# Attention operands turned through DRAM by one write and one read, with the keys in another order on the partitions

## The chip, the core and the metric

The kernel runs on one core of one Trainium2 chip. The metric is the device time of one execution in microseconds (us). It is given as the median of the timed runs; beside it there is one profiled execution with its trace, whose own time and span are given below.

## The reference, cut to what matters

The model is a decoder trunk of two layers over 272 tokens (16 learned "meta" tokens and 256 of the sequence), with a width of 2048, 16 heads of 128 and an MLP of 8192. Layer 0 is a softmax attention with a forget gate, layer 1 a stick-breaking attention.

```python
for qs, qe in query_blocks(L):          # (0,16), (16,144), (144,272)
    s = einsum('bqhd,bkhd->bhqk', q[:, qs:qe], k[:, :qe]) * scale + decays   # layer 0
    p = softmax(where(mask, s, -inf))
    out = einsum('bhqk,bkhd->bqhd', p, v[:, :qe])
    # layer 1: a = exp(log_sigmoid(z) + suffix sums of log_sigmoid(-z)), strictly causal, out = a @ v
h = h + out @ w_o
h = h + square(relu(rms_norm(h) @ w_up)) @ w_down        # in both layers
```

The sum over the keys k in the last `einsum` doesn't depend on the order in which the keys are taken, as long as the probabilities and the values are in the same order.

## The kernel before, in words

**Layout.** The residual stream is kept with features on the partitions (`hT`, 16 chunks of 128 features by 272 tokens). Every large product is split into parts of reduced precision: a weight block becomes `whi` (L210, on ScalarE, ACT) and `wlo` (L211, on VectorE, DVE), an activation becomes `sp.hi` and `sp.lo`, and three products are summed in place of one (hi·hi, hi·lo, lo·hi).

**Groups.** `gemm_group` makes 512 output features: four blocks of 512 contracted features (`kb` 0 to 3), four output chunks (`m`), four chunks of 128 (`kc`) in a block and three products make 192 products on TensorE (PE). The groups are counted by `u`: 1 to 12 are q, k and v of layer 0 (for four sets `g` of four heads), 13 to 16 its output projection, 17 to 48 its MLP, 49 to 52 the queries of layer 1, 53 to 60 its keys and values, 61 to 64 its output projection and 65 to 96 its MLP. With `t0 = 16` (u = 49 to 52 and from 61) a product is 256 tokens wide, in the others 272. Some products are "widened": they take `sp.wide`, which has 6 columns of zeros behind the 256, so that they write 262 columns, of which 256 are read.

**Attention.** The scores of a head come out with queries on the partitions. The product with the values needs the keys there, for the probabilities and for the values. Both are turned in two steps: VectorE transposes blocks of 32 by 32 (L474, L389), and a trip through DRAM moves the blocks to their partitions. For a pair of heads `pr` (two pairs in a set of four heads), `turn_probabilities` writes to `p_dram[pr]` and `probabilities_back` reads it into `raw`; `scratch` writes to `v_dram[pr]` and `values_read` reads it back into the same tile `turned`. Before the change each write is four DMAs, one for each quarter `a` of the partitions, and the read is one DMA of 2 KB (values) or 3 KB (probabilities) in a row for each partition. Then `values_back` splits the values (`v0` by L377 on ACT and L378 on DVE, `v1` by L409 on ACT). Only when these are done can `weighted` and L812 (L618 in layer 0) make `po` on PE. After that L822 adds the share of the last 16 keys (`own`, copied by L818 on ACT) and `put_split` writes the heads' chunks of `ao` (named x_o; L466 on ACT, L467 on DVE), which the output projection reads.

**The last heads.** The attention of the last four heads of a layer has no later group of its own kind to lie in. It lies in the first group of the output projection (u = 13 and u = 61), at places that are written out by hand: `last_heads(turned, reads, uses, places, ...)` gives the product numbers behind which the values are read, behind which they are split, and at which the two pairs of heads stand on PE. Products 144 to 191 of that group (`kb` = 3) read the chunks of just these heads: chunks 12 and 13 (the first pair) from product 144 on, chunks 14 and 15 (the second pair) from product 168 on.

**The order.** A scheduler sets the order on each engine at build time; `behind` ties a DMA or a split to a place among the products. Each engine works in that order. A DMA that reads from DRAM waits on its issuing queue (POOL's, SP's or ACT's) until the write has landed, and all that is issued behind it waits too. Small pieces (the meta tokens, the last 16 keys) go through `c_dram` and `m_dram` on the same queues.

Of the kernel before, what the change touches and what calls it, by code (L numbers as in the profile page):

```python
# [33 lines left out]
def yoco_kernel(ctx: ExitStack, tc: tile.TileContext, hT_in, gains, b_f, w_f, w_qkv0, w_o0, w_up, w_dn,  # L34
# [180 lines left out]
    def gemm_group(wblk, sp, t0, evac, before={}, after={}, load_x=None, between={}):  # L215
# [7 lines left out]
        for kb in range(4):  # L223
# [16 lines left out]
            for kcs, ms in runs:  # L240
# [6 lines left out]

                wide = [(0, 0, 0), (1, 0, 1), (2, 1, 1)] if t0 and u % 4 == 1 else []
                if u == 61:
# [142 lines left out]
    def scratch(t, products, queues=(nc.gpsimd, nc.gpsimd)):  # L392
        for pr in range(2):
            y = t[:, pr].rearrange("p (c x) -> p c x", c=4)
            for a in range(4):
                ins = queues[pr].dma_start(v_dram[pr].rearrange("c j a x -> a j c x")[a], y[32 * a:32 * a + 32])
                behind(ins, products[pr])

    def values_read(t, pr, read, queue=nc.gpsimd):
        ins = queue.dma_start(t[:, pr], v_dram[pr].rearrange("c j a x -> (c j) (a x)"))  # L400
        behind(ins, read)
        return ins.ins
# [66 lines left out]
    def turn_probabilities(s, raw, pr, queue):  # L469

        y = raw[:, :768].rearrange("p (c h b i) -> p c h b i", c=4, h=2, b=3)
        for i in range(2):
            for b, o in enumerate((0, 144, 144 + P)):
                nc.vector.transpose(y[:, :, i, b, :], s[:, 2 * pr + i, o:o + P].rearrange("p (c k) -> p c k", c=4))  # L474
        y = y.rearrange("p c h b i -> p c (h b i)")
        for a in range(4):
            queue.dma_start(p_dram[pr].rearrange("c j a x -> a j c x")[a], y[32 * a:32 * a + 32])

    def probabilities_back(pps, places, queue):
        for pr, at in enumerate(places):  # L480
            raw, p0 = pps[pr]
            behind(queue.dma_start(raw[:, :768], p_dram[pr].rearrange("c j a x -> (c j) (a x)")), issued[at])

# [258 lines left out]
    for g in range(4):  # L742
# [43 lines left out]
        turned = squares(vT, "pp", f"1_{g}")  # L786
        if g < 3:
            scratch(turned, issued[-2:])
        else:
            scratch(turned, (issued[-20], issued[-1]), (nc.gpsimd, nc.scalar))  # L790

# [47 lines left out]

    box["last"] = last_heads(turned, (36, 60), (84, 116), (120, 146), "1_3", nc.gpsimd, pair1, corner1)  # L840

# [11 lines left out]
    def to_token_major():  # L853
        t = squares(hT[:, 12:, M:], "pp", "h")
        scratch(t, issued[-2:])
        return t
# [131 lines left out]
```

## Time and profile before

| | us |
|---|---|
| median of 3 runs | 2265.85 (2265.61 to 2266.42) |
| profiled execution, its own time | 2264.61 |
| span of that execution's trace | 2262.9 |
| busy: PE, PE weight load | 2255.1, 2247.0 |
| busy: DVE, ACT, POOL | 1355.1, 1056.6, 120.5 |
| DMA | 435.94 MB, 193 GB/s in the mean |

The profile is one execution. Its page gives the busy time of each engine, the time slice by slice, and the chain of work that ended last; the trace behind it answers by line, by tile, by wait and in order of time. In an answer in order of time a row has the start, the time until the last of its instructions ended, the engine, the line of the kernel and the operation, `out<-in`, and in brackets the idle time ahead of it and what ended that. PE's instructions overlap, so that a run of products goes forward by less than the sum of their durations; it is read from one start to the next.

### The profile page before, as it was taken

The numbers are of one execution on the slowest core, as the hardware profiler recorded it, in microseconds if no ns is written. First come the engines' busy times: TensorE is split into PE (matmuls) and PEld (weight loads), VectorE is DVE, ScalarE is ACT, GpSimd is POOL, SyncE is SP. The second block draws the span as 40 slices with busy tenths as digits, with TensorE's granted clock in tenths as the row PEclk, the third lists the DMA queues.
The fourth block names the chain that finished last, engine by engine and source line by source line (L and its number), as shares of the span: only waits on it lengthen the run. The fifth ranks groups of instructions, "written<-read, shape, count | busy, mean of one in ns | idle before, by whom it ended". The sixth has DMA issues, their size and how long they took to land.

```text
span 2262.9 us, 45001 instructions
## 1 busy us (share of the span) xinstructions
PE 2255.1 (100%) x18785; PEld 2247.0 (99%) x18785; DVE 1355.1 (60%) x1989; ACT 1056.6 (47%) x1440; POOL 120.5 (5%) x236
## 2 busy tenths in 40 slices
PE   9999999999999999999999999999999999999998
PEld 9999999999999999999999999999999999999998
DVE  7777676554455455455566688766555555555555
ACT  6444445453354344344444455555544543543554
POOL 1321210000000000000000011200000000001001
PEclk9999999999999999999999999999999999999999
DMA  7766765555555555555555566665656656566664
GB/s 242 238 201 192 227 208 170 186 169 184 179 177 180 175 176 185 173 184 178 170 192 183 180 220 219 213 218 188 198 186 197 198 192 197 186 197 209 197 199 141
DMA packets 131852, 435.94 MB, mean 193 GB/s; under 512 B 18528, under 2 KB 26352, under 8 KB 131648
## 3 DMA queue, kind: packets, MB, share of 16 engines
q1 hardware_dynamic: 122112, 413.57, 56.1%
q0 software_dynamic: 6640, 15.80, 2.3%
q10 hardware_dynamic: 2896, 3.69, 0.5%
q8 instruction: 147, 2.41, 0.4%
q14 instruction: 57, 0.47, 0.1%
HBM read 419.22 MB, written 13.78 MB: 191 GB/s over the span
## 4 chain that ended last, share of the span: by engine, by line
PE 98%; DMA 1%; DVE 0%; issue 0%; ACT 0%; POOL 0%; SPq 0%; POOLq 0%; ACTq 0%
PE acc L177 96%; PE po L415 0%; PE pz L415 0%; PE ps L415 0%; DMA raw<-w_o 0%; DMA turned<-v_dram 0%; DMA raw<-w_qkv 0%; PE pz L764 0%; PE ps L541 0%; DVE wlo L211 0%; PE po L618 0%; PE po L812 0%; ACT whi L210 0%; PE pf L346 0%; POOL ob L887 0%
## 5 line engine op out<-in xcount | busy, mean ns | idle before, releaser
L211 DVE TENSOR_TENSOR wlo<-raw,whi 128x1024 fp32r<-128x1024 f32 (+1 forms) x774 | 928.4, 1215 | 693.1 <-ACT whi L210 685.9
L210 ACT ACTIVATE whi<-raw 128x1024 fp32r<-128x1024 f32 (+1 forms) x774 | 796.7, 1049 | 984.6 <-PE acc L177 947.3
L177 PE MATMUL acc<-x_m,whi 128*128 128x272 f32 (+1 forms) x4096 | 642.9, 281 | 0.0
L177 PE MATMUL acc<-x_u,whi 128*128 128x272 f32 (+1 forms) x3968 | 626.0, 281 | 0.0
L177 PEld LDWEIGHTS acc<-x_m,whi 128*128 128x128 f32 x4096 | 565.7, 188 | 0.1
L177 PEld LDWEIGHTS acc<-x_u,whi 128*128 128x128 f32 x3968 | 550.1, 188 | 0.0
L177 PE MATMUL acc<-x_m,wlo 128*128 128x272 f32 (+1 forms) x2048 | 440.7, 281 | 0.0
L177 PE MATMUL acc<-x_u,wlo 128*128 128x272 f32 (+1 forms) x1984 | 431.5, 281 | 0.0
L177 PE MATMUL acc<-x_a,whi 128*128 128x272 f32 (+1 forms) x2048 | 352.3, 285 | 0.2 <-ACT whi L210 0.2
L177 PEld LDWEIGHTS acc<-x_m,wlo 128*128 128x128 f32 x2048 | 323.2, 188 | 0.0
L177 PEld LDWEIGHTS acc<-x_u,wlo 128*128 128x128 f32 x1984 | 315.1, 188 | 0.0
L177 PEld LDWEIGHTS acc<-x_a,whi 128*128 128x128 f32 x2048 | 300.2, 188 | 1.5 <-issue 0.9
L177 PE MATMUL acc<-x_a,wlo 128*128 128x272 f32 (+1 forms) x1024 | 252.9, 285 | 0.0
L177 PE MATMUL acc<-x_kv,whi 128*128 128x272 f32 x1024 | 193.2, 288 | 0.0
L177 PEld LDWEIGHTS acc<-x_a,wlo 128*128 128x128 f32 x1024 | 175.4, 188 | 0.6 <-issue 0.4
L177 PE MATMUL acc<-x_o,whi 128*128 128x272 f32 (+1 forms) x1024 | 162.4, 282 | 0.5 <-ACT x_o L466 0.3
L177 PEld LDWEIGHTS acc<-x_kv,whi 128*128 128x128 f32 x1024 | 160.7, 188 | 0.0
L177 PE MATMUL acc<-x_kv,wlo 128*128 128x272 f32 x512 | 146.9, 287 | 0.0
L177 PEld LDWEIGHTS acc<-x_o,whi 128*128 128x128 f32 x1024 | 142.1, 188 | 0.8 <-ACT x_o L466 0.5
L295 DVE TENSOR_TENSOR hT<-acc,hT 128x272 f32<-128x272 f32 (+1 forms) x156 | 67.3, 432 | 73.2 <-PE acc L177 73.0
L177 PE MATMUL acc<-x_o,wlo 128*128 128x272 f32 (+1 forms) x512 | 110.4, 281 | 0.0
L177 PEld LDWEIGHTS acc<-x_kv,wlo 128*128 128x128 f32 x512 | 96.4, 188 | 0.0
(221 smaller groups left out, 1120.9 us busy)
## 6 DMA issues: line engine op xcount, KB each, us to landing
raw<-w_up SPq DMA_DIRECT2D x256, 512.0 KB, 4.0
raw<-w_dn SPq DMA_DIRECT2D x256, 512.0 KB, 4.3
raw<-w_qkv SPq DMA_DIRECT2D x92, 512.0 KB, 4.4
raw<-w_o SPq DMA_DIRECT2D x64, 512.0 KB, 4.4
raw<-w_kv SPq DMA_DIRECT2D x64, 512.0 KB, 4.3
raw<-w_q SPq DMA_DIRECT2D x32, 512.0 KB, 4.3
v_dram<-turned POOLq DMA_DIRECT2D x56, 64.0 KB, 3.9
turned<-v_dram POOLq DMA_DIRECT2D x14, 256.0 KB, 5.3
```

The costliest lines, as they stand in the source:

```text
L177: ins = nc.tensor.matmul(*args, **kw).ins
L210: on_act = nc.scalar.activation(hp, src, AF.Copy)
L211: on_dve = nc.vector.tensor_tensor(out=lp, in0=src, in1=hp.bitcast(F32), op=ALU.subtract)
L295: nc.vector.tensor_tensor(out=hT[:, c, t0:], in0=acc, in1=hT[:, c, t0:], op=ALU.add)
```

## The change

Four things change. (1) In both trips through DRAM (`scratch` with `values_read`, `turn_probabilities` with `probabilities_back`) the write is one DMA over all 128 partitions in the order in which they lie, and the read picks four pieces (512 bytes each for values, 768 for probabilities) for each partition; the keys come to lie on the partitions as (j c) and no longer (c j). The trip of the final tokens (`to_token_major`) keeps the four writes and the old order. (2) The write of the last heads' second pair in layer 1 goes to POOL's queue; before, it went to ACT's. (3) The places of the last heads of layer 1 change: splits behind products 70 and 106 (before: 84 and 116), pairs at 112 and 132 (before: 120 and 146). (4) Seven more products are widened: three in u = 62, two each in u = 49 and u = 65.

```diff
@@ -245,7 +245,9 @@
                     products = [(kc, m, *pair) for m in ms for kc in kcs for pair in pairs]
                 left = {m: 3 * len(kcs) for m in ms}
 
-                wide = [(0, 0, 0), (1, 0, 1), (2, 1, 1)] if t0 and u % 4 == 1 else []
+                wide = [(0, 0, 0), (1, 0, 1), (2, 1, 1)] if t0 and (u % 4 == 1 or u == 62) else []
+                if t0 and 2 in before:
+                    wide = wide + [(2, 0, 0), (2, 1, 0)]
                 if u == 61:
                     wide = wide + [(3, 2, 0), (3, 2, 1), (3, 3, 1)]
                 for kc, m, part, x in products:
@@ -391,13 +393,11 @@
 
     def scratch(t, products, queues=(nc.gpsimd, nc.gpsimd)):
         for pr in range(2):
-            y = t[:, pr].rearrange("p (c x) -> p c x", c=4)
-            for a in range(4):
-                ins = queues[pr].dma_start(v_dram[pr].rearrange("c j a x -> a j c x")[a], y[32 * a:32 * a + 32])
-                behind(ins, products[pr])
+            ins = queues[pr].dma_start(v_dram[pr].rearrange("a j c x -> (a j) (c x)"), t[:, pr])
+            behind(ins, products[pr])
 
     def values_read(t, pr, read, queue=nc.gpsimd):
-        ins = queue.dma_start(t[:, pr], v_dram[pr].rearrange("c j a x -> (c j) (a x)"))
+        ins = queue.dma_start(t[:, pr].rearrange("p (a x) -> p a x", a=4), v_dram[pr].rearrange("a j c x -> (j c) a x"))
         behind(ins, read)
         return ins.ins
 
@@ -472,14 +472,12 @@
         for i in range(2):
             for b, o in enumerate((0, 144, 144 + P)):
                 nc.vector.transpose(y[:, :, i, b, :], s[:, 2 * pr + i, o:o + P].rearrange("p (c k) -> p c k", c=4))
-        y = y.rearrange("p c h b i -> p c (h b i)")
-        for a in range(4):
-            queue.dma_start(p_dram[pr].rearrange("c j a x -> a j c x")[a], y[32 * a:32 * a + 32])
+        queue.dma_start(p_dram[pr].rearrange("a j c x -> (a j) (c x)"), raw[:, :768])
 
     def probabilities_back(pps, places, queue):
         for pr, at in enumerate(places):
             raw, p0 = pps[pr]
-            behind(queue.dma_start(raw[:, :768], p_dram[pr].rearrange("c j a x -> (c j) (a x)")), issued[at])
+            behind(queue.dma_start(raw[:, :768].rearrange("p (a x) -> p a x", a=4), p_dram[pr].rearrange("a j c x -> (j c) a x")), issued[at])
 
     def split_probabilities(raw, p0):
         return split(p0.rearrange("p x i q -> p x (i q)").rearrange("p x (m y) -> p x m y", m=8),
@@ -784,10 +782,7 @@
         gemm_group(w_kv[2 * g + 1], xc, 0, lambda m, acc: evac_kv(m, acc, vT))
         probabilities_back(pps, (140, 184), nc.sync)
         turned = squares(vT, "pp", f"1_{g}")
-        if g < 3:
-            scratch(turned, issued[-2:])
-        else:
-            scratch(turned, (issued[-20], issued[-1]), (nc.gpsimd, nc.scalar))
+        scratch(turned, issued[-2:] if g < 3 else (issued[-20], issued[-1]))
 
         def corner1(pm_sb, read=None, g=g, vT=vT, pps=pps):
             for pr in range(2):
@@ -837,7 +832,7 @@
                 own1(box["small"], product)
             finish1(pr, po, box["small"][3])
 
-    box["last"] = last_heads(turned, (36, 60), (84, 116), (120, 146), "1_3", nc.gpsimd, pair1, corner1)
+    box["last"] = last_heads(turned, (36, 60), (70, 106), (112, 132), "1_3", nc.gpsimd, pair1, corner1)
 
     xm, norm_m = out_proj(w_o1, ao, M, G_M1, "m1", box.pop("last"))
 
@@ -852,7 +847,10 @@
 
     def to_token_major():
         t = squares(hT[:, 12:, M:], "pp", "h")
-        scratch(t, issued[-2:])
+        for pr in range(2):
+            y = t[:, pr].rearrange("p (c x) -> p c x", c=4)
+            for a in range(4):
+                behind(nc.gpsimd.dma_start(v_dram[pr].rearrange("c j a x -> a j c x")[a], y[32 * a:32 * a + 32]), issued[-2 + pr])
         return t
 
     def tokens_back(t):
```

The new form of the trip lets the scheduler order some instructions in another way. Three places follow. In the rows a name ends in the buffer's numbers.

On POOL, at the last heads of layer 1 (the tile `turned_3`, its DRAM buffers `v_dram_156` for the first pair and `v_dram_157` for the second, and between them the small pieces `pmq_3` and `pk_vc_3`), before:

```order
L440 DMA c_dram<-pkT_3_16875 32x4x16
L120 CAST x_m_17147<-pad 128x16x6
L396 DMA v_dram_156<-turned_3_17129 32x4x128 x4
L445 DMA pmq_3_17259<-c_dram 128x16
L433 COPY pk_vc_3_17268<-vT_3_16878 128x4x16 x2
L400 DMA turned_3_17129<-v_dram_156 128x512
L400 DMA turned_3_17129<-v_dram_157 128x512
```

The same place on POOL now:

```order
L440 DMA c_dram<-pkT_3_16785 32x4x16
L120 CAST x_m_17051<-pad 128x16x6
L396 DMA v_dram_156<-turned_3_17039 128x512
L445 DMA pmq_3_17163<-c_dram 128x16
L433 COPY pk_vc_3_17172<-vT_3_16788 128x4x16 x2
L396 DMA v_dram_157<-turned_3_17039 128x512
L400 DMA turned_3_17039<-v_dram_156 128x4x128
L400 DMA turned_3_17039<-v_dram_157 128x4x128
```

The first pair's write is one row and no longer four DMAs; the second pair's write, which stood on ACT, stands behind the two copies `pk_vc_3`, and both reads come after it.

On PE, in u = 61, around the second pair of the last heads (`po_3_1`, between the products with `whi` and `wlo` of block `kb`_half), before:

```order
L177 MATMUL acc_2_17151<-x_o_14583,wlo_2_1_17300 128x256
L177 MATMUL acc_3_17152<-x_o_14583,wlo_2_1_17300 128x256
L415 MATMUL po_3_1_17389<-p_3_1_16861,v_1_3_1_17384 128x256 x3
L812 MATMUL po_3_1_17389<-raw_p_3_1_16853,v_1_3_1_17385 128x128
L415 MATMUL po_3_1_17389<-p_3_1_16861,v_1_3_1_17384 128x256 x3
L812 MATMUL po_3_1_17389<-raw_p_3_1_16853,v_1_3_1_17385 128x128
L177 MATMUL acc_0_17149<-x_o_14583,whi_3_0_17374 128x256
L177 MATMUL acc_1_17150<-x_o_14583,whi_3_0_17374 128x256
```

And now:

```order
L177 MATMUL acc_2_17055<-x_o_14535,whi_2_1_17203 128x256
L177 MATMUL acc_3_17056<-x_o_14535,whi_2_1_17203 128x256
L415 MATMUL po_3_1_17267<-p_3_1_16774,v_1_3_1_17262 128x256 x3
L807 MATMUL po_3_1_17267<-raw_p_3_1_16766,v_1_3_1_17263 128x128
L415 MATMUL po_3_1_17267<-p_3_1_16774,v_1_3_1_17262 128x256 x3
L807 MATMUL po_3_1_17267<-raw_p_3_1_16766,v_1_3_1_17263 128x128
L177 MATMUL acc_0_17053<-x_o_14535,whi_2_1_17203 128x256
L177 MATMUL acc_1_17054<-x_o_14535,whi_2_1_17203 128x256
```

The second pair stood behind product 143, right ahead of block 3; it now stands behind product 131, twelve products ahead of that block. The first pair stands behind product 111; before, it began behind product 120 and was cut in two by ten products.

On POOL, behind the first set of heads of layer 0 (`turned_0`, and the trip of the meta tokens through `m_dram` to `vm_sb`), before:

```order
L396 DMA v_dram_157<-turned_0_1206 32x4x128 x4
L445 DMA pmq_0_943<-c_dram 128x16
L433 COPY pk_vc_1199<-vT_0_161 128x4x16 x2
L400 DMA turned_0_1206<-v_dram_156 128x512
L460 DMA m_dram<-vt_0_1488 32x8x32 x4
L400 DMA turned_0_1206<-v_dram_157 128x512
L462 DMA vm_sb_1202<-m_dram 128x2x128
```

And now:

```order
L445 DMA pmq_0_937<-c_dram 128x16
L426 COPY pk_vm_1191<-vT_0_161 128x128
L433 COPY pk_vc_1193<-vT_0_161 128x4x16 x2
L396 DMA v_dram_157<-turned_0_1200 128x512
L400 DMA turned_0_1200<-v_dram_156 128x4x128
L400 DMA turned_0_1200<-v_dram_157 128x4x128
L460 DMA m_dram<-vt_0_1476 32x8x32 x4
L462 DMA vm_sb_1196<-m_dram 128x2x128
```

Both reads of the values stand ahead of the four writes to `m_dram` now. On PE the product that reads `vm_sb` (`pom`, L600) stands at the start of u = 5; before, it stood behind 33 products of that group.

## The prediction, made before the changed kernel was run

> **What bounds the kernel now.** I read the page first. TensorE is busy for the whole span, and the chain of work that ended last is TensorE's own.
>
> ```profile
> PE 2255.1 (100%) x18785; PEld 2247.0 (99%) x18785; DVE 1355.1 (60%) x1989; ACT 1056.6 (47%) x1440; POOL 120.5 (5%) x236
> ...
> PE 98%; DMA 1%; DVE 0%; issue 0%; ACT 0%; POOL 0%; SPq 0%; POOLq 0%; ACTq 0%
> ```
>
> Since a busy PE can hide short stops, I asked next for PE's waits.
>
> ```profile
> PE idle L61 <- DVE mean_w L57: 1.1, 1, 1.1
> PE pr_fin L177 <- DVE fin L900: 0.8, 1, 0.8
> PE acc L177 <- ACT x_o L466: 0.3, 1, 0.3
> PE acc L177 <- ACT whi L210: 0.2, 1, 0.2
> PE acc L177 <- DVE x_o L467: 0.2, 1, 0.2
> ```
>
> All waits come to 2.6 us. The first two are the start and the tail, which the change doesn't touch. Two are for x_o: the output projection of layer 1 waits for its last heads. The chain in order of time gives the pace of the products.
>
> ```profile
> 423.83 756.84 PE acc L177 x6144
> 1567.20 671.86 PE acc L177 x5891
> ```
>
> That is 756.84 / 6144 = 0.123 us for a product of 272 columns and 671.86 / 5891 = 0.114 us for one of 256. With this pace I looked for lost time in PE's rows in order of time, in u = 61, from its first product to the place behind the last heads.
>
> ```profile
> 1464.43 1.08 PE L177 MATMUL acc<-x_o,whi 128*128 128x262 f32 x8
> ...
> 1481.43 1.07 PE L177 MATMUL acc<-x_o,wlo 128*128 128x256 f32 x8
> 1482.47 0.84 PE L415 MATMUL po<-p,v 128*128 128x256 f32 x3
> ...
> 1484.38 1.18 PE L177 MATMUL acc<-x_o,whi 128*128 128x256 f32 x8 [0.26 <-ACT x_o L466]
> 1485.75 1.18 PE L177 MATMUL acc<-x_o,whi 128*128 128x256 f32 x8 [0.20 <-DVE x_o L467]
> ```
>
> A pair that waits for nothing is seen in a middle group of layer 1, from its first product to the next pair's:
>
> ```profile
> 1324.79 0.52 PE L415 MATMUL po<-p,v 128*128 128x256 f32 x3
> ...
> 1325.87 0.48 PE L415 MATMUL po<-p,v 128*128 128x256 f32 x2
> ```
>
> There a pair takes 1.08 us. In u = 61 the eight products from 1481.43 should take 0.91 and take 1.04 (0.13 lost), the pair takes 1.91 (0.83 lost), and the eight products from 1484.38 take 1.37 (0.46 lost): 1.42 us in all. This is the only place found where PE stands still for anything the change touches, so 1.42 us is about the most that it can bring.
>
> **Why PE stands there.** ACT's rows at that place:
>
> ```profile
> 1467.31 2.83 ACTq L396 DMA_DIRECT2D v_dram<-turned  x4
> ...
> 1482.00 0.42 ACT L377 ACTIVATE v<-turned 128x256 fp32r<-128x256 f32 x1 [2.48 <-DMA turned<-v_dram]
> 1482.33 0.39 ACT L409 COPY v<-turned 128x256 f32<-128x256 f32 x1
> 1482.62 0.26 ACT L818 COPY own<-pvc 128x128 f32<-128x128 f32 x1
> 1482.78 1.06 ACT L210 ACTIVATE whi<-raw 128x1024 fp32r<-128x1024 f32 x1
> 1483.74 0.58 ACT L466 ACTIVATE x_o<-po 128x512 fp32r<-128x512 f32 x1
> ```
>
> DVE's:
>
> ```profile
> 1482.91 0.23 DVE L822 TENSOR_TENSOR po<-po,own 128x64 f32<-128x64 f32 x1
> 1483.87 1.23 DVE L211 TENSOR_TENSOR wlo<-raw,whi 128x1024 fp32r<-128x1024 f32 x1 [0.72 <-ACT whi L210]
> 1485.01 0.69 DVE L467 TENSOR_TENSOR x_o<-po,x_o 128x512 fp32r<-128x512 f32 x1
> ```
>
> And POOL's:
>
> ```profile
> 1465.43 2.20 POOL L396 DMA_DIRECT2D v_dram<-turned  x4 [0.50 <-DVE turned L389]
> ...
> 1468.38 0.91 POOL L433 COPY pk_vc<-vT 128x64 f32<-128x64 f32 x2
> ...
> 1476.76 0.55 POOL L400 DMA_DIRECT2D turned<-v_dram  x1 [4.99 <-DVE wlo L211]
> ```
>
> The second pair's values are written from ACT (1467.31 to 1470.14), read from 1476.76 and there at 1482.00. The copy of `own` comes only behind them, and the first pair's x_o behind that: so PE waits first for values, then for x_o.
>
> **Part 1, the last heads of layer 1 (the large term).** On POOL the first write is one DMA (0.55 us in place of 2.20). The copies still end at 1468.38 + 0.91 = 1469.29; the second pair's write follows until 1469.84, then the reads. How long write and read take, and how long a read stood behind its write in the middle group:
>
> ```profile
> v_dram<-turned POOLq DMA_DIRECT2D x56, 64.0 KB, 3.9
> turned<-v_dram POOLq DMA_DIRECT2D x14, 256.0 KB, 5.3
> ```
>
> ```profile
> 1311.67 2.17 POOL L396 DMA_DIRECT2D v_dram<-turned  x4
> ...
> 1319.34 0.57 POOL L400 DMA_DIRECT2D turned<-v_dram  x1 [4.94 <-DMA v_dram<-turned]
> ```
>
> At the best the write lands 3.9 after 1469.29, at 1473.2; at the worst as in the middle group, where the read began 5.5 us after the last write was issued: 1475.3. A read in 512 pieces is not in the trace. Its issue is bounded below by today's 0.55 and above by four writes of 128 pieces (2.20); the nearest rows are DMAs of 256 pieces:
>
> ```profile
> L460 POOL DMA_DIRECT2D m_dram<-vt x12 | 7.1, 592 | 14.3 <-issue 7.6 <-DVE pm_sb L449 6.6
> ...
> L462 POOL DMA_DIRECT2D vm_sb<-m_dram x3 | 2.1, 709 | 13.0 <-DMA m_dram<-vt 13.0
> ```
>
> I take 1.0 us, 0.45 more than now. With 5.3 for the read, the second pair's values arrive between 1473.2 + 5.3 = 1478.5 and 1475.3 + 5.8 = 1481.1; I take 1480.
>
> PE reaches product 112 at 1464.43 + 112 x 0.114 = 1477.2. The first pair's read starts by 1469.84 and is there by about 1475.6; its splits (0.42, 0.39 and 0.42 on DVE) end by 1476.9, so nothing is lost. With 1.08 for the pair, some 0.25 for `own` and 20 products (2.28), PE reaches product 132 at 1480.8, and needs split values there. From 1480 ACT splits until 1480.8 and DVE a little longer: about 0.1 lost. Twelve products behind the pair PE is at 1483.4 and wants x_o of the first pair. ACT gets there by copy, a `whi` (1.06, now ahead of `own`), `own` (0.26), L822 (0.23) and L466 (0.58): 1480.8 + 2.1 = 1482.9, in time. The low part waits behind a `wlo` on DVE: 1482.4 + 1.23 + 0.69 = 1484.3, and is wanted eight products on, at 1484.3. The second pair's x_o has 36 products of cover where it had 24. So I leave 0.4 us of the 1.42: **-1.0 us**; ends 0 (values at 1481.5 or later) and -1.42.
>
> The Trainium skill, "DMA: Bandwidth & Descriptors", section "Anatomy of one DMA — SWDGE (gpsimd) path", fits such a DMA as about 2.0 us plus bytes over 436 GB/s. For 256 KB that would be 2.6 us, an estimate from the page; the trip would be over by 1475 and the term -1.42. The row of 5.3 us beside a running weight stream says twice that, and the sum goes by the row.
>
> **Part 2, the other trips.** In the other seven sets of heads PE waits for nothing now; a trip that ends sooner brings 0. The same bytes move; writes come in larger pieces, reads in smaller ones. What hides them is the distance to the use: in the middle group the second read was issued at 1319.34 for a pair at 1325.87. If that cover went, each us of delay beyond it would cost one. On SP four issues become one ahead of the same read, which lets the weight loads behind it go sooner. 0.
>
> **Part 3, the widened products.** Seven of them, 6 columns more each. In proportion that is 0.003 us each, at most the step to the 272 pace, 0.009: +0.02 to +0.06, taken as +0.05. They wait for nothing.
>
> **Sum.** -1.0 + 0.05 = -0.95 us. Against the profiled execution's own 2264.61 (its span is 2262.9) that is 2263.7. The median of the runs shown stands 1.24 above that execution, so the forecast is 2265.85 - 0.95 = **2264.9 us**. A difference of 0.2% (4.5 us) is about what a measurement of this kernel can tell from no change; this one is smaller.
>
> **Rivals.** *The values are no earlier.* The second write, now behind the copies, is issued at 1469.3 and no longer from 1467.31, in a stretch where the weight loads run; if it and a read of 512 pieces take 12 us together, PE stands as long as before. For it speak the 5.5 us of the middle group, against it that ACT's four issues themselves lasted to 1470.14. Time: 2265.85 + 0.05 = 2265.9. The Trainium skill, "DMA: Bandwidth & Descriptors", section "Issuing engines are not separate DMA queues", holds that another issuing engine saves only the issue time. By that rule the move from ACT to POOL alone would give this outcome, and no run so far separates the two queues' transfers.
>
> *Slower: the first set of layer 0.* Its `pom` product needs `vm_sb`:
>
> ```profile
> 87.61 2.20 POOL L396 DMA_DIRECT2D v_dram<-turned  x4 [0.54 <-DVE wlo L211]
> ...
> 108.55 0.71 POOL L462 DMA_DIRECT2D vm_sb<-m_dram  x1 [4.88 <-DMA m_dram<-vt]
> ```
>
> ```profile
> 111.73 0.33 PE L600 MATMUL pom<-s0T,vm_sb 128*128 128x64 f32 x2
> ```
>
> ```profile
> m_dram<-vt POOLq DMA_DIRECT2D x12, 32.0 KB, 4.2
> ...
> vm_sb<-m_dram POOLq DMA_DIRECT2D x3, 128.0 KB, 3.3
> ```
>
> `pom` now stands 33 products (4.07 us) sooner, at 107.66, so `vm_sb` has to be issued by 107.66 - 3.3 = 104.4, 4.2 us sooner than before. The second write goes out near 90 now (it was 87.61; a small read and two copies stand ahead), lands at 94 to 95.5, the second read takes 1.0, the four `m_dram` writes 4 x 0.592, and the last lands 4.2 later: 101 to 103.5. That leaves 1 to 3 us. Were the reads issued in 2.2 us each and the landings at the 5.5 of the middle group, it would be near 107, and PE would stand for 2.5 us: 2264.9 + 2.5 = 2267.4. It decides from 105.4 on, where it eats the gain.
>
> *Slower: the last pair's new place.* Product 132 comes at 1480.8, 1.7 us ahead of the old start of the pair. If the small pieces made the read land after 1482, PE would lose more than before; at 1484, some 1.7 us more: 2267.6.
>
> *Faster by over 0.2%* would need 4.5 us, and all of PE's waits are 2.6.
>
> **The numbers.** Forecast 0.62, values no earlier 0.2, layer 0 0.1, the new place 0.08. The first reaches from -1.42 with the runs' scatter of 0.3 (2264.1) to 2265.5; the rivals reach to 2267.6. I give 2264.0 to 2267.2, which leaves out the far parts of the last two. All cases lie within 4.5 us of 2265.85 except a sum of several delays: faster 0.02, within 0.2% 0.93, slower 0.05.
>
> **What would show it.** In the trace after: ACT's second L377 of u = 61 near 1480 to 1481 and not at 1482; PE's waits for x_o gone or under 0.2 us; u = 61 shorter by about 1 us (from its first product to that of u = 62); POOL's L400 with a duration of 0.55 to 1.0. Wrong would be: a wait of PE at `pom` of u = 5 or at `po` of any set, a second read that lands after 1481.5, or products of 262 columns that go at more than 0.123 us.

## The result, and the profile after

The forecast was 2264.9 us, and 0.93 lay on "within 0.2%". The kernel after takes **2293.16 us** (median of 4 runs, 2289.97 to 2294.50); before, on the same chip, 2265.79 (4 runs). The ratio is 1.0118, 95% interval 1.0102 to 1.0134: slower by about 27 us. The profiled execution takes 2293.87 us with a span of 2292.1, which is 29.2 more than the 2262.9 of before.

The page of the kernel after, busy times and the chain that ended last by engine and by line:

```profile
PE 2265.7 (99%) x18785; PEld 2255.2 (98%) x18785; DVE 1352.4 (59%) x1989; ACT 1057.0 (46%) x1440; POOL 89.2 (4%) x171
...
PE 91%; DMA 4%; issue 3%; DVE 1%; POOL 1%; SPq 0%; ACT 0%; POOLq 0%; ACTq 0%; DVEq 0%
```

Where the chain was 98% PE, it now leaves PE for DMAs and for "issue", which is time in which an engine waits for nothing that the profile shows. PE's waits in the kernel after (us in total, times, longest):

```profile
PE pom L598 <- DMA vm_sb<-m_dram: 14.7, 3, 5.8
PE po L415 <- ACT v L379: 2.1, 1, 2.1
...
PE po L415 <- DVE v L380: 0.8, 1, 0.8
...
PE acc L177 <- ACT whi L210: 0.6, 1, 0.6
PE acc L177 <- DVE vT L503: 0.6, 1, 0.6
```

Three waits at `pom`, one for each of the first three sets of layer 0, are the bulk. The time of a group, from its first product to that of the next in PE's rows, says where the 29.2 us lie:

| groups | before, us | after | what is in them |
|---|---|---|---|
| u = 1 | 27.17 | +1.29 | first weights, untouched by the change |
| u = 4, 5 | 51.13 | +6.32 | heads of the first set |
| u = 6, 7 | 51.79 | +8.82 | heads of the second set, in u = 7 |
| u = 9, 10 | 51.79 | +7.02 | heads of the third set, in u = 10 |
| u = 11 to 13 | 76.88 | +1.22 | last heads of layer 0 in u = 13 |
| u = 55, 57, 59 | 78.74 | +2.24 | middle groups of layer 1 |
| u = 61 | 25.99 | +2.49 | last heads of layer 1 |
| MLPs, u = 17 to 48 and 65 to 96 | | under 0.05 | |

**The long waits.** PE in order of time at the first set, then the granted clock there (the windows' columns are length, busy time of PE, PEld, DVE, ACT and POOL with their instructions, PEclk, DMA share, GB/s):

```profile
108.68 0.29 PE L177 MATMUL acc<-x_a,wlo 128*128 128x272 f32 x1
113.46 0.43 PE L598 MATMUL pom<-s0T,vm_sb 128*128 128x64 f32 x2 [4.50 <-DMA vm_sb<-m_dram]
...
113.94 0.99 PE L415 MATMUL po<-p,v 128*128 128x256 f32 x3
...
117.14 0.69 PE L415 MATMUL po<-p,v 128*128 128x256 f32 x3
```

```profile
104.00:108.60 4.60, 4.60 (x40) 4.60 (x39) 3.30 (x6) 1.61 (x5) 1.46 (x3) 1.00 0.78 248
108.60:113.40 4.80, 0.37 (x3) 0.15 (x2) 3.65 (x7) 1.54 (x2) 2.54 (x2) 1.00 0.36 134
113.40:117.10 3.70, 3.64 (x19) 3.64 (x20) 1.79 (x6) 1.20 (x4) 0.17 (x1) 0.57 0.77 265
```

PE stands for 4.5 us, and then the clock is granted at 0.57 for the next 3.7: the heads' products, three in 0.99 us here, take 0.69 once it is back. So 4.5 us of waiting cost the two groups 6.3. With the waits of 5.8 and 4.4 us in the next two sets the clock stands at 0.50 for 6.83 us each (from 195.84 and from 281.17), and their groups lose 8.82 and 7.02. The Trainium skill, "TensorE: Matmul & The Clock Gate", section "Part 1: The HAM clock gate (the "warmup" mystery)", states such a drop to half rate after an idle stretch of about 3.4 us. The half rate agrees; the length doesn't hold as a bound here: the clock also fell to 0.50, for 3.41 us, with the wait of 2.13 us in u = 61 and behind one of 1.65 us in m_first, and it stayed at 1.00 behind one of 3.36 us in before_read512, at u = 55 (both kernels are among the experiments below).

**What `pom` waits for.** POOL in order of time at the first set:

```profile
91.75 0.76 POOL L400 DMA_DIRECT2D turned<-v_dram  x1 [1.56 <-DMA v_dram<-turned]
97.88 0.75 POOL L400 DMA_DIRECT2D turned<-v_dram  x1 [5.37 <-issue]
98.63 0.61 POOL L460 DMA_DIRECT2D m_dram<-vt  x1
103.72 1.73 POOL L460 DMA_DIRECT2D m_dram<-vt  x3 [4.48 <-issue]
110.86 0.72 POOL L462 DMA_DIRECT2D vm_sb<-m_dram  x1 [5.40 <-DMA m_dram<-vt]
```

A read in 512 pieces is issued in 0.76 us, but the DMA behind it stands 5.37 us, and the second `m_dram` write 4.48 more, for nothing that the profile shows. The landings in the trace (issue plus the time to landing) tell more. The second read's own write landed at 95.02; the read went out at 97.88, 0.36 us after the first read had landed (97.52). The second `m_dram` write went out at 103.72, 0.31 us after the second read had landed (103.41). In all seven sets in which a second read stands for "issue" it goes out 0.34 to 0.37 us after the first read has landed, and 2.0 to 7.2 us after its own write has: POOL holds the next DMA until an earlier one is through. The part of the stand up to the landing of its own write would be there without this. Over the whole kernel (groups of instructions; busy time and mean, then idle time ahead and what ended it):

```profile
L400 POOL DMA_DIRECT2D turned<-v_dram x14 | 10.7, 762 | 48.5 <-issue 44.2 <-DMA v_dram<-turned 2.4 <-PE acc L177 1.8
...
L460 POOL DMA_DIRECT2D m_dram<-vt x12 | 7.0, 591 | 13.6 <-issue 13.6
```

The reads before:

```profile
L400 POOL DMA_DIRECT2D turned<-v_dram x14 | 7.8, 560 | 22.7 <-DMA v_dram<-turned 17.3 <-DVE wlo L211 5.0 <-issue 0.3
```

They stood 0.3 us for "issue". `vm_sb` goes out at 110.86, 25.7 us after the start of u = 4; before it went out at 108.55, 24.6 us after it, for a `pom` that stood 33 products later. In set two it goes out 27.2 us after the start of u = 7, where it was 16.0 before: 11.2 us later, when PE has already reached the end of the group's 192 products (before: product 130).

**DVE.** A second thing in the trace is the multiplication of `pm_sb` in the second set:

```profile
166.82 0.29 DVE L449 TENSOR_TENSOR pm_sb<-pmq,maskD 128x128 f32<-128x128 f32 x1 [5.25 <-DMA pmq<-c_dram]
...
168.16 0.43 DVE L503 TENSOR_TENSOR vT<-acc,rstd_a 128x272 f32<-128x272 f32 x1
```

DVE stands 5.25 us for a trip through `c_dram`, and the copies of the values out of PSUM (`vT`) and their transposes stand behind it. Before, that multiplication stood behind all four copies and all but the last transposes, and didn't wait in this set. The diff doesn't name it: the scheduler put it there.

**u = 61.** POOL, ACT and PE at the last heads (u = 61 begins at 1491.20, 26.77 later than before):

```profile
1496.01 0.55 POOL L396 DMA_DIRECT2D v_dram<-turned  x1
1496.55 0.75 POOL L400 DMA_DIRECT2D turned<-v_dram  x1
1503.23 0.76 POOL L400 DMA_DIRECT2D turned<-v_dram  x1 [5.94 <-issue]
```

```profile
1509.55 0.42 ACT L379 ACTIVATE v<-turned 128x256 fp32r<-128x256 f32 x1 [4.82 <-DMA turned<-v_dram]
```

```profile
1510.02 1.04 PE L415 MATMUL po<-p,v 128*128 128x256 f32 x3 [2.13 <-ACT v L379]
```

The same stand again: the second read is held 5.94 us, its values come at 1509.55, and PE waits for them at the new place.

### The profile page after: what moved, and what is told of

Same layout as the page of the kernel before. It is cut to its first block, busy times and chain, and to the rows that moved or that the text cites. A ratio compares the mean times of both kernels' runs of the same rounds, so it can differ in the third digit from the quotient of the medians.

```text
span 2292.1 us, 44823 instructions
## 1 busy us (share of the span) xinstructions
PE 2265.7 (99%) x18785; PEld 2255.2 (98%) x18785; DVE 1352.4 (59%) x1989; ACT 1057.0 (46%) x1440; POOL 89.2 (4%) x171
## 4 chain that ended last, share of the span: by engine, by line
PE 91%; DMA 4%; issue 3%; DVE 1%; POOL 1%; SPq 0%; ACT 0%; POOLq 0%; ACTq 0%; DVEq 0%
PE acc L177 88%; DMA pmq<-c_dram 1%; DMA v_dram<-turned 1%; DMA m_dram<-vt 1%; PE po L415 1%; DMA hT<-hT_in 0%; DMA p_dram<-raw_p 0%; DVE wlo L211 0%; DMA vm_sb<-m_dram 0%; DMA turned<-v_dram 0%; PE ps L415 0%; PE pz L415 0%; PE po L616 0%; POOL m_dram L460 0%; DVE vT L503 0%
```

## The experiments

In the tables of groups below, the numbers are the profiled execution's loss against the 2262.9 of before, read as in the table above. Times and ratios are medians and 95% intervals against the kernel before on the same chip (2265.8 to 2267.0).

### First: room, pieces, or order

The word "issue" at POOL suggested room. The Trainium skill, "DMA: Bandwidth & Descriptors", section "SWDGE vs HWDGE vs iDMA", has the descriptors of POOL's DMAs appended to a ring in SBUF, and those of SP and ACT made by hardware. The kernel sets 1024 bytes of a partition for POOL's (`dynamic_dma_scratch_size`). SBUF is full, so for a larger room two masks of layer 0 were put into a tile that layer 1 uses.

```diff
-    maskA = const.tile([P, 416], F32, name="maskA")
+    goes_on = const.tile([P, 2, 416], F32, name="goes_on")
+    maskA = goes_on.rearrange("p i k -> p (i k)")[:, :416]      # maskM beside it, goes_on filled after layer 0
...
-    nc = bacc.Bacc(..., dynamic_dma_scratch_size=1024)
+    nc = bacc.Bacc(..., dynamic_dma_scratch_size=3072)
```

> The kernel after, with one number changed: the room for the descriptors of POOL's DMAs is 3072 bytes of a partition and no longer 1024 (to make place in SBUF, the masks of layer 0 share a tile with one of layer 1, which is filled again between the layers; nothing else moves). Theory A (room): a read in 512 pieces needs four times the descriptors of the old read, and POOL stands at its next DMA until earlier ones have left. Then the 44.2 us that POOL stands at `turned` for 'issue' go to under 10, the 14.7 us at `pom` to under 3, and the time comes to 2264.5 to 2268. Theory B (drain): small pieces leave slowly whatever the room, and what is queued behind them waits in the queue instead of on POOL: POOL's waits for 'issue' go, but `m_dram` lands as late as now, the wait at `pom` stays at 10 us or more, and the time stays at 2285 to 2294. Theory C (order: both reads now stand ahead of the `m_dram` writes, and each waits for its own write to land): POOL's wait moves from 'issue' to the landing of `v_dram`, and the time stays above 2280.

> The kernel before with the same change of room and masks, as the control: PE waits for nothing there that POOL issues, so all theories expect 2265.5 to 2266.2. The fourth `m_dram` write, which stood 1.84 us for 'issue' in the first set, should follow the third at once by theory A, and still stand by B and C.

```diff
     def values_read(t, pr, read, queue=nc.gpsimd):                          # read128, on the kernel after
-        ins = queue.dma_start(t[:, pr].rearrange("p (a x) -> p a x", a=4), v_dram[pr].rearrange("a j c x -> (j c) a x"))
+        ins = queue.dma_start(t[:, pr], v_dram[pr].rearrange("c j a x -> (c j) (a x)"))
```

> The kernel after, in which the values are read back in 128 pieces of 2 KB again, the writes staying as they are (so the values arrive in a wrong order and the heads' outputs are not the reference's; order of instructions and bytes are the same as in the kernel after). Theory A: each read takes a quarter of the descriptors; the waits at `turned` for 'issue' go to under 5 us, `pom` waits under 3, the time is 2264.5 to 2269. Theory B expects the same within 2 us, since the pieces are gone. Theory C: the order is untouched, so `pom` waits 10 us or more and the time stays above 2280.

```diff
-            rows_turned([vm, vc], vm_sb, issued[112], issued[130], f"0_{g}")             # m_on_sp
+            rows_turned([vm, vc], vm_sb, issued[112], issued[130], f"0_{g}", nc.sync)
```

> The kernel after, in which the four `m_dram` writes of each set of layer 0 are issued from SP's queue (as those of layer 1 are) and not from POOL's; the reads stay in 512 pieces. Theory A: POOL no longer stands at `m_dram` (13.6 us for 'issue' go), and the writes no longer wait behind the second read; `vm_sb` is issued 5 us or more sooner, the wait at `pom` goes to under 3 us, and what is left is u = 61: 2266.5 to 2271. Theory B: the writes no longer queue behind the pieces in one queue, so it expects the same or a little more, up to 2275. Theory C: as A, since the writes pass the reads. If SP's queue itself, which stands for free weight buffers, holds the writes back, the time stays above 2285.

| | us | ratio | u = 4, 5 | 6, 7 | 9, 10 | u = 61 |
|---|---|---|---|---|---|---|
| after | 2293.2 | 1.0118 (1.0102 to 1.0134) | +6.32 | +8.82 | +7.02 | +2.49 |
| ring3072 | 2277.5 | 1.0047 (1.0031 to 1.0063) | +6.06 | +3.57 | +2.92 | -0.24 |
| before_ring3072 | 2266.5 | 0.9999 (0.9989 to 1.0008) | 0.00 | 0.00 | 0.00 | +1.55 |
| read128 | 2284.6 | 1.0079 (1.0063 to 1.0094) | +6.03 | +5.83 | +7.38 | -1.15 |
| m_on_sp | 2284.0 | 1.0072 (1.0052 to 1.0091) | +8.17 | +2.49 | +1.06 | +3.23 |

Room is real. With 3072 bytes POOL no longer stands for "issue" in the kernel after (0.4 us, where it was 44.2); these are the kernel's reads (its line numbers are two lower) and its first waits of PE:

```profile
L398 POOL DMA_DIRECT2D turned<-v_dram x14 | 10.6, 760 | 25.5 <-DMA v_dram<-turned 23.4 <-PE acc L175 1.7 <-issue 0.4
```

```profile
PE pom L596 <- DMA vm_sb<-m_dram: 5.7, 3, 3.3
PE acc L175 <- DVE vT L501: 4.1, 4, 1.4
```

The control agrees at the place it was made for: in the kernel before, the fourth `m_dram` write of the first set stood 1.84 us for "issue", and with 3072 it stands 0.23 at most. Rows of before, then of its twin with the larger room:

```profile
98.88 1.79 POOL L460 DMA_DIRECT2D m_dram<-vt  x3 [6.56 <-DVE pm_sb L449]
102.51 0.60 POOL L460 DMA_DIRECT2D m_dram<-vt  x1 [1.84 <-issue]
```

```profile
99.29 0.62 POOL L458 DMA_DIRECT2D m_dram<-vt  x1 [6.93 <-DVE pm_sb L447]
100.14 1.75 POOL L458 DMA_DIRECT2D m_dram<-vt  x3 [0.23 <-issue]
```

The word "issue" alone doesn't prove a lack of room, though: at its reads the control shows 7.0 us of it where before had 0.3. Of these, 1.34 us is a stand that ends 0.54 us after the read's own write has landed, and 5.16 us stand where before had a wait of 5.29 us for that landing: the word also covers waits for a landing that the profile doesn't name. What shows the room is the pair of kernels, and the landings above.

But theory A alone fell: it expected 2264.5 to 2268 and got 2277.5. About half of the stand became a wait for the landing of the read's own write, as theory C had it (23.4 us), though C's time, above 2280, wasn't met either; that kernel is still slow in the first set. In read128 the short reads no longer stand, yet `pom` waits 10.9 us, and the time is where C said. Its rows at the first set show why: both reads are ahead of `m_dram`, and the fourth write has no room again.

```profile
97.11 1.82 POOL L460 DMA_DIRECT2D m_dram<-vt  x3
103.54 0.59 POOL L460 DMA_DIRECT2D m_dram<-vt  x1 [4.62 <-issue]
```

In m_on_sp the expectation of 2266.5 to 2271 failed too: POOL still stands 41.4 us at the reads, and `vm_sb` behind them. What is common to all is the first set, at +6 or more. So room was one cause of several.

### Second: the place, the order, the wait on DVE

```diff
         gemm_group(w_qkv0[3 * g + 1], xa, 0, ..., after={j: (lambda j=j: decays(j)) for j in range(4)},
+                   between={33: heads} if g == 1 else {})      # pom33: small_outputs and pairs of set 0 as `heads`
```

> The kernel after with one thing put back: in the first set of layer 0 the products `pom` and `po` stand behind product 33 of u = 5 on PE, as before the change, and no longer ahead of product 0. Theory P (place): 4.07 us of the first set's loss come from the place alone; its wait falls from 4.7 to about 0.6 us, u = 4 and 5 together lose under 2 us where they lost 6.3, and the time is 2287 to 2289.5. Theory L (landing only: the wait would follow the place, since what `vm_sb` waits for is itself released by PE): the wait stays above 3 us and the time at 2291 to 2294. Sets two and three, where `pom` stood at product 0 before the change too, stay as they are by both.

```diff
-            for pr in range(2):
-                values_read(turned, pr, issued[100 + 10 * pr])                              # m_first
+            values_read(turned, 0, issued[100])
...                                                               # the second read: issued[131], behind the m_dram writes
```

> The kernel after with POOL's order in layer 0 put back: the second values' read stands behind the four `m_dram` writes, as before the change, and not ahead of them. Theory O (order and room together): each `m_dram` write then stands behind one full read and not two; `vm_sb` is issued about 7 us sooner, the waits at `pom` of sets two and three (6.0 and 4.6 us) go to under 1 and that of the first to under 2; the second read is later instead and `po` may wait 1 to 3 us a set; time 2270 to 2280. Theory A (room alone): the first read alone fills the room, `m_dram` is issued no sooner than now, and the time stays above 2287.

```diff
         turned = squares(vT, "s", f"0_{g}")
+        behind(box["spread"](), issued[-1])          # ring_pm: the multiplication of pm_sb, until then in corner_back
```

> The kernel with 3072 bytes of room (2277.5 us), in which DVE multiplies `pm_sb` behind the transposes of the values again, as before the change, and not ahead of them, in layer 0. Theory D (DVE): the wait for `pmq` (27.8 us in 8 waits) stood in DVE's queue ahead of the copies out of PSUM (`vT`) and the transposes; with it behind them PE's waits for `vT` (4.1 us in 4) go to under 1, the values' writes go out 1 us sooner and the waits at `pom` shrink from 5.7 to 3 to 5; time 2270.5 to 2274. If the copies were late for another reason, the waits for `vT` stay above 3 us and the time at 2276 to 2278.

> The same with `pom` of the first set behind product 33 of u = 5 too. If room, place and the wait on DVE are all there is to layer 0, u = 4 to 13 lose under 3 us together (they lost 23 in the kernel after and 14 with room alone), and the time is 2265.5 to 2268.5; if the order on POOL (both reads ahead of `m_dram`) costs on its own, waits at `pom` of sets two and three of 1 us and more are left and it is 2269 to 2273.

| | us | ratio | u = 4, 5 | 6, 7 | 9, 10 | u = 11 to 13 | u = 61 |
|---|---|---|---|---|---|---|---|
| pom33 | 2294.8 | 1.0122 (1.0099 to 1.0145) | -0.01 | +6.35 | +9.05 | +1.85 | +1.60 |
| m_first | 2279.7 | 1.0060 (1.0043 to 1.0077) | +3.47 | +2.21 | +0.75 | +1.11 | +3.75 |
| ring_pm | 2271.0 | 1.0019 (1.0010 to 1.0028) | +1.01 | 0.00 | 0.00 | +0.01 | -0.57 |
| ring_pm_pom | 2265.9 | 0.9998 (0.9989 to 1.0008) | +0.90 | +1.11 | 0.00 | +0.01 | -0.35 |

This is the chain of the cause. Room brings the kernel after from 1.0118 to 1.0047, `pm_sb` back behind the copies from there to 1.0019, and `pom` behind product 33 to 0.9998: the whole loss, in three steps, the last two as expected. The third step stands in the medians alone: the profiled execution of ring_pm was the fastest of ten (2266.1, median 2271.0), so its groups show too small a loss, and u = 4 and 5 look alike in both traces (+1.01 and +0.90). DVE's wait for `pmq` is gone from the critical place: PE's waits for `vT` no longer appear, and `pom` waits 0.8 us in one set.

```profile
PE pom L604 <- DMA vm_sb<-m_dram: 0.8, 1, 0.8
```

The steps aren't independent. In pom33, with the small room, the first set is whole in the trace (-0.01), and still the median is no better than after, above what either of its two theories gave. In its trace sets two and three together lose about as much as after (15.4 and 15.8), and that execution was the fastest of four (2287.6; the others 2293.0 to 2300.5). The order on POOL counts as well: with the second read behind `m_dram`, as before the change, 13 us come back with the small room (1.0118 to 1.0060), though `po` then waits 3.0 us for the later values in u = 61, a group that this edit doesn't touch.

### Third: the pieces alone, and what the others cost with the small room

```diff
-        ins = queue.dma_start(t[:, pr], v_dram[pr].rearrange("c j a x -> (c j) (a x)"))     # before_read512, on the kernel before
+        ins = queue.dma_start(t[:, pr].rearrange("p (a x) -> p a x", a=4), v_dram[pr].rearrange("a j c x -> (j c) a x"))
```

> The kernel before, in which only the values' reads of the heads are cut into 512 pieces of 512 bytes (writes, places and queues as before the change; the values arrive in a wrong order, so the heads' outputs are not the reference's). POOL's order keeps `m_dram` between the two reads. Theory A (pieces and room): POOL stands for 'issue' at `m_dram` and at the second reads, 20 us and more in all, `vm_sb` goes out about 5 us later than the 176.54 and 252.68 of before, of which 4.3 were spare: PE stands 0 to 2 us a set, u = 61 loses 1 to 3: 2268 to 2274. If pieces cost only together with the new order, PE waits nowhere and the time is 2265.5 to 2267.5.

The kernels pm_pom, ring_pm_pom_oldplaces and ring_pm_pom_mfirst are combinations of the edits above, the second with one more:

```diff
-    box["last"] = last_heads(turned, (36, 60), (70, 106), (112, 132), "1_3", nc.gpsimd, pair1, corner1)
+    box["last"] = last_heads(turned, (36, 60), (84, 116), (120, 146), "1_3", nc.gpsimd, pair1, corner1)
```

> The kernel after with the small room (1024), `pm_sb` behind the transposes and `pom` of the first set behind product 33: what the room costs alone, beside the 2265.9 of the same kernel with 3072. Sets two and three keep a wait of 3 to 5 us each at `pom`, u = 55 to 61 lose 3 to 5 us together as in the kernel after, u = 4 and 5 under 2: 2277 to 2285. If room only costs together with the wait on DVE, the time is under 2270.

> The kernel with 3072 bytes of room, `pm_sb` and `pom` put back (2265.9 us), with the old places of the last pairs of layer 1 (values split behind products 84 and 116, pairs at 120 and 146). If the new places bring what the prediction said, u = 61 is 0.5 to 1.2 us longer than in the kernel with the new ones (25.64 by its trace), near the 25.99 of before; the time, 2266 to 2267.5, can't tell it. If the new places were what cost 2.5 us in the kernel after, u = 61 gets shorter, to 25.3 or less.

> All four: 3072 bytes of room, `pm_sb` and `pom` put back, and the second values' read of layer 0 behind the `m_dram` writes. If POOL's order still costs with room for all, the last waits at `pom` (0.8 us) go and the time is 2264.5 to 2265.9, as forecast for the change itself; if the later second read costs more, `po` waits 0.5 us and more a set and it is 2266.5 to 2269.

| | us | ratio | layer 0 (u = 4 to 13) | u = 55 to 60 | u = 61 |
|---|---|---|---|---|---|
| before_read512 | 2279.0 | 1.0057 (1.0043 to 1.0070) | +6.36 | +6.71 | +3.16 |
| pm_pom | 2283.5 | 1.0073 (1.0050 to 1.0095) | +5.60 | +2.46 | +0.26 |
| ring_pm_pom_oldplaces | 2267.8 | 1.0008 (0.9999 to 1.0017) | +0.19 | -0.12 | -1.09 |
| ring_pm_pom_mfirst | 2265.3 | 0.9997 (0.9989 to 1.0006) | 0.00 | -0.12 | +0.72 |

Cutting the reads in pieces, with the old writes, order, places and queues, costs 13 us by itself; the expectation (2268 to 2274) had left out the middle groups of layer 1. PE waits in that kernel for values, once in each of four groups of layer 1 (u = 55, 57, 59 and 61), and twice at `pom` in layer 0:

```profile
PE po L415 <- ACT v L377: 8.7, 4, 3.4
PE pom L600 <- DMA vm_sb<-m_dram: 4.3, 2, 2.8
```

Of pm_pom the profiled execution was the fastest (2273.48; the others 2283.49 to 2289.34), so its groups show too small a loss; the median says that room alone costs 17 us once the other two are put back. The fastest of these kernels, ring_pm_pom_mfirst, comes out at 0.9997, about where the forecast had put the change; that can't be told from no change, and in its trace u = 61 is 0.72 us longer than before, so it doesn't bear out the forecast's reason.

### Fourth: whose descriptors, and the places

```diff
-                values_read(turned, pr, issued[100 + 10 * pr])                              # reads_act, on pm_pom
+                values_read(turned, pr, issued[100 + 10 * pr], nc.scalar)
```

> The kernel with small room and with `pm_sb` and `pom` put back (2283.5 us), in which the values' reads of layer 0, in 512 pieces as they are, are issued by ACT's hardware queue. Theory A (room for POOL's own descriptors): they take none of it, POOL's stands for 'issue' at `turned` of layer 0 (about 7 us a set) go, and u = 6 to 10 lose under 1 us where they lost 5.5 by its trace; layer 1 stays as it was; time 2268 to 2274. Theory B (small pieces are slow for the DMA engines whoever issues them): `m_dram` stays late and the time above 2278.

> The kernel after with the small room, in which only `pm_sb` of layer 0 stands behind the transposes again. If DVE's wait alone costs what it did with large room (the copies of room gained 6.5 us by it), the waits for `vT` go and those at `pom` shrink by 1 to 2 us each: 2285 to 2290. If it only pays once the room is there, 2291 to 2294.

> The kernel after with the small room, in which only the last pairs of layer 1 have their old places again (values split behind products 84 and 116, pairs at 120 and 146). With small room the second values land some 6 us late (1509.5 in the trace after), so the later place gives 14 products, 1.6 us: u = 61 loses 0.5 to 1.5 us where it lost 2.5; the rest is untouched, and the time is 2288 to 2294. If the place made no difference there, u = 61 loses 2.5 still.

The last kernel is ring_pm_pom_mfirst with the old places:

> A version that might beat both kernels: the one trip in two DMAs with 3072 bytes of room, `pm_sb`, `pom` and the second read of layer 0 put back, and the old places in layer 1. By the trace with the old places u = 61 takes 24.9 us, 1.1 less than before: 2264.3 to 2265.8, if the kernel before gives 2265.9 to 2266.5; more than 1.4 us of gain isn't there by any theory.

| | us | ratio | layer 0 (u = 4 to 13) | u = 55 to 60 | u = 61 |
|---|---|---|---|---|---|
| reads_act | 2271.1 | 1.0023 (1.0013 to 1.0032) | 0.00 | +5.85 | +0.31 |
| pm_only | 2291.7 | 1.0124 (1.0104 to 1.0144) | +24.89 | +1.65 | +0.86 |
| old_places | 2300.8 | 1.0149 (1.0131 to 1.0166) | +29.97 | +5.49 | +4.41 |
| best | 2268.3 | 1.0012 (1.0003 to 1.0020) | +1.70 | -0.12 | +2.56 |

With the layer-0 reads in ACT's queue, in the same 512 pieces and with the small room, layer 0 loses nothing; what is left is layer 1, whose reads stayed on POOL. POOL's reads in that kernel:

```profile
L400 POOL DMA_DIRECT2D turned<-v_dram x8 | 6.1, 764 | 29.8 <-issue 24.4 <-PE acc L177 2.7 <-DMA v_dram<-turned 2.6
```

Eight reads are left on POOL and stand 24.4 us. So it isn't the small pieces that are slow wherever they come from (theory B), but POOL's descriptors for them. One reservation: the edit also takes the reads out of POOL's order, ahead of `m_dram`, which is worth something by m_first, so the share of each in the 12 us gained (2283.5 to 2271.1) isn't shown.

That agrees with the ring of the Trainium skill's section above: the reads on POOL stood 44.2 us for "issue" in the kernel after and 0.4 with three times the room.

pm_only with the small room brings nothing (1.0124): while POOL is late, putting the multiplication back on DVE doesn't help. old_places came out above its expectation (2288 to 2294), through layer 0, which the edit doesn't touch: in its trace `pom` waits 19.0 us in three sets. u = 61 loses 4.41 there and not 0.5 to 1.5, so that expectation failed too; with the small room the old places don't help. The kernel meant to beat both didn't: 1.0012, with a wait of 1.9 us in u = 61 for x_o.

**Open.** What the new places of the last pairs are worth could not be settled. With large room u = 61 lost -0.24, -0.57, -0.35 and +0.72 us with the new places, -1.09 and +2.56 with the old ones, and +1.55 in the kernel before; the differences between executions are larger than the term. The medians lean to the new places: with them the same kernel is faster in both pairs (0.9998 against 1.0008, and 0.9997 against 1.0012, some 2 and 3 us), but the intervals overlap, and in the second pair 1.69 of the loss lies in layer 0 by the trace. Open is also u = 1, 0.8 to 1.5 us longer in ten of the fifteen traces made from the kernel after and -0.2 to 0.5 in the others.

## Why the prediction was wrong, point by point

- **What bounds the kernel: right.** PE did, its 1.42 us in u = 61 was about all there was to gain, and no kernel was faster than before by more than its interval.
- **Part 3, the widened products: right.** u = 49 takes 22.285 us in place of 22.272, u = 65 22.246 in place of 22.233, two such products each: 0.0065 us apiece, 0.046 for seven (said: +0.05).
- **Part 1, up to the first read: right to 0.1 us.** Less the 26.77 us, the second write goes out at 1469.24 (said 1469.29) and the first read at 1469.78 (1469.84). The second write lands at 1473.91, inside the 1473.2 to 1475.3 that were said. **The issue of a read: the step that failed.** The issue itself takes 0.76 us, less than the 1.0 that was taken. But that was taken for all that the read costs its queue. Behind a read of 512 pieces POOL stands until there is room: the second read goes out at 1476.46, 6.7 us after the first and 2.55 after its own write has landed, and takes 6.3 us to land where 5.3 was taken from the row. So the values come at 1482.78 where 1480 was said. The sign stood in a row that the prediction shows: `m_dram`, writes of 256 pieces, with 7.6 us of "issue" in the kernel before. It was read for the price of an issue alone. The bound of 1481.1 also adds 5.8 us for a read where the row says 5.3, without a reason. With room for the descriptors they came at 1479.31 in ring_pm_pom_oldplaces, whose u = 61 begins 0.5 us later than that of before; the time of the values was right there, the size of the gain stays open.
- **Part 2, the other trips = 0: wrong, and the largest miss.** "PE waits for nothing now" was true, but the cover was read in a middle group of layer 1 alone, and the term was put at 0. In set two of layer 0 `vm_sb` went out at 176.54 and landed 3.4 us later, for a `pom` at 184.22: 4.3 us of cover, gone when it went out 11.2 us later in its group; in set three it went out 10.2 us later. In place of 0, layer 0 lost 23.4 us in the trace (u = 4 to 13) and the middle groups of layer 1 lost 2.2. The queue behind the reads was what had to be priced: four `m_dram` writes and `vm_sb`. Two of the prediction's own signs of being wrong came with it: a wait at `pom` of u = 5, and second values later than 1481.5.
- **Rival "first set of layer 0": right mechanism and place, mis-sized.** It had `pom` 33 products sooner and `vm_sb` near 107; it went out at 110.86, or 109.7 less the 1.1 us by which u = 4 begins later. Its 2.5 us were priced for one set at full clock. The wait was 4.5 us, the clock fell to 0.57 behind it (6.3 in all), and two more sets, which no rival had, lost more still. It had a chance of 0.1.
- **Not seen at all: `pm_sb` on DVE.** The multiplication was moved ahead of the copies `vT` by the scheduler, and its wait for a trip held the copies that PE waits for. Putting it back is worth 6.3 us with large room (1.0047 to 1.0019).
- **Rival "the last pair's new place": its condition came true** (values after 1482, and u = 61 lost 2.49 us in the trace), but for the reason above and not for the small pieces.

## What to carry to other kernels

A DMA costs its queue more than its own issue: count the pieces that stand behind each other on POOL against the room for descriptors, and the instructions that are queued behind them. An unexplained "issue" on a queue in the profile of before is a reason to ask what holds it: see whether the next DMA goes out just after an earlier one lands. Fewer, larger writes that are paid with four times as many pieces in the read were no gain here; if a read has to be scattered, try it on a queue whose descriptors hardware makes (ACT's here), or make the room. And when a trip gets "sooner" in a scheduler's eyes, look for what it moves up on the other engines: a wait that was hidden may now stand in front of the bound.

## What the runs showed of the hardware that was not expected

- The room of 1024 bytes a partition held at least 896 pieces that hadn't landed yet, and not 1024. In read128 a read of 128 and three writes of 256 went out one behind the other, and the fourth write stood 4.62 us. In the kernel after, a second read of 512 stood behind a first that hadn't landed; with one read of 512 and one write of 256 out, the next 256 stood 4.48. In the kernel before, the fourth write behind three of 256 stood 1.84. Each went on 0.3 to 0.4 us after an earlier DMA had landed. With 3072 bytes neither the read nor the writes stood.
- A wait of 4.5 us on PE cost 6.3, because the clock was granted at 0.57 for 3.7 us behind it; how long the clock stays down varied from one wait to the next (0, 3.41 and 6.83 us at 0.50 with waits of 3.36, 1.65 and 4.40 us).
- Kernels that wait scatter: pm_pom ran from 2273.5 to 2289.3 and pom33 from 2287.6 to 2300.5, where the kernel before kept within 5.1 us in the runs beside each.
